# Seven-product MLP blocks: weight sums written later, products reordered, additions spread, transposes given a second PSUM pool

## The chip, the core and the metric

One core of a Trainium2 chip runs the whole program. The metric is device time in microseconds of one execution; the median of three runs is given, and beside it one further execution was profiled. Engines are named as in the profile: PE is the matrix engine (PEld its weight loads), DVE the vector engine, ACT the scalar engine, SP the engine whose queue issues the weight loads from HBM.

## The reference

A trunk of two layers on 256 tokens of width 2048. Each layer has a token mixer (differential attention in the first, a Mamba-2 mixer in the second) and then a squared-ReLU MLP with 8192 hidden units; both are pre-normed and added to the residual. The change touches the two MLPs only.

```python
def rms_norm(x, gain):
    y = xf * lax.rsqrt(jnp.mean(xf * xf, axis=-1, keepdims=True) + EPS)
    return y * gain
def sq_relu_mlp(h, w1, w2):
    return jnp.square(jax.nn.relu(h @ w1)) @ w2
...
for i in range(DEPTH):                      # DEPTH = 2
    hn = rms_norm(h, mixer_norm[i])
    h = h + (diff_attention(hn, ...) if i % 2 == 0 else mamba2_mixer(hn, ...))
    h = h + sq_relu_mlp(rms_norm(h, mlp_norm[i]), mlp_w1[i], mlp_w2[i])
```

All arrays are float32.

## The kernel before

**Precision.** Every operand of a matrix product is split in two: a rounded high part (a cast on ACT) and the rest (a subtraction on DVE). `split_weights` does it for a 128x1024 tile of weights (lines 158 and 159), `split_pair` for activations (lines 263 and 264). A product then takes high by high, high by low and low by high, three matmuls where one would do. So each 512 KB tile of weights costs one load (SP), one cast (ACT, L158), one subtraction (DVE, L159) and 12 or 6 wide matmuls.

**Stages.** Attention, first MLP (`mlp0`, about 405 to 1075 us in the profile), Mamba-2 mixer, second MLP (`mlp1`, about 1760 us to the end). The hidden layer of an MLP is made in eight chunks of 1024 columns. `MLP_KINDS` is "sSSSSSSS": chunk 0 is made by plain blocks (`blocks`, lines 169 and 173), the other seven by `seven`, a Strassen-Winograd product of 2x2 blocks with seven half-size products in place of eight. `seven` reads four quarters of a weight chunk, in four row parts i each: `src[0]` is B11, `src[1]` B12, `src[2]` B22, `src[3]` B21. It works in three loops over i:

- first loop: P1 = A11 B11 and P5 = S1 (B11 - B12), the sum kept in a tile `wsum` (L569);
- second loop: P7 = S3 (B22 - B12) (L579), P3 = S4 B22, P6 = S2 (B22 + wsum) (L584);
- third loop: P2 = A12 B21 and P4 = A22 (wsum - B21) (L600).

Each product of one i is six wide matmuls (L557 and L559) into one PSUM bank. The banks come from three pools: `aux` has three banks, `aux1` one, and `mm` (called by `bank()`) four, which the second matrix uses. After the second loop five additions (L587 to L591) form three of the four output quarters from P1, P3, P5, P6 and P7, and four ACT instructions (L593, L594) apply the squared ReLU to two of them; after the third loop L603 and L604 finish the other two, with L606 and L607.

**Second matrix.** `expand` turns a finished chunk `u` into transposed, split activations: for chunk 0 four splits only, for the others four groups of four PE transposes (L656), each group into an `aux` bank, and then a split out of that bank. `token_steps` multiplies them by tiles of w2 (L238, L240).

**Order.** The MLP goes in four quarters q. While quarter q is multiplied by w2, the two chunks of quarter q+1 are made: after each w2 step some `yield`s of the generator `seven` are taken (`work`, `rate`). The first two chunks are made together (`both(0, ...)`): four yields of `blocks`, then the two in turn. I call that stage the first pair. Small work hangs in a queue (`side`), of which `side.tick()` runs one step. Within an engine a scheduler of the framework settles the final order of instructions from this recording, so a line that is written later need not stand later. All waits between engines are by semaphores, and a tile's buffer (`raw` 5, `w` 4, `wsum` 4) is used again when its last reader is done.

## Time and profile before

| | |
|---|---|
| median of three runs | 2449.77 us (2448.08 to 2452.68) |
| the profiled execution | 2449.62 us, of which the span of the profile is 2447.9 us |
| granted PE clock | 1.0 throughout |
| PE busy | 2434.1 us, 99% of the span |
| DVE busy | 2098.2 us, 86% |
| ACT busy | 1535.6 us, 63% |
| DMA | 500.54 MB, mean 204 GB/s |

How to read it: a row of a group of instructions gives the engine, the operation, tiles written and read, the shape, the count, busy time in us and mean time of one in ns, and then the idle time of the engine just ahead of these instructions with what ended it. A row of the timeline gives start and duration in us, and in brackets idle time and its releaser. Matmuls overlap: a 512-column matmul is recorded with 0.39 us but the next can start 0.23 us after it. So I speak of PE by the distance of two starts, not by its busy time.

### The profile page before, as it was taken

What the parts mean: (1) busy time and instruction counts of PE and PEld (TensorE: products, weight loads), DVE (VectorE), ACT (ScalarE), POOL (GpSimd) and SP (SyncE); (2) the same over time, 40 slices, a digit from 0 to 9 for tenths busy, and PEclk for the clock granted to TensorE, in tenths of its full rate; (3) what the DMA queues carried; (4) which work ended last, traced back from release to release, by engine and by line L of the source; (5) the groups of instructions that cost most, each with busy time, mean ns of one, the idle gap of its engine ahead of it and who ended that gap; (6) DMA issues with size and microseconds to landing.
All of it is one profiled execution on the core that took longest, in us unless ns stands there. A gap on an engine that the chain in (4) does not pass through costs nothing.

```text
span 2447.9 us, 32626 instructions
## 1 busy us (share of the span) xinstructions
PE 2434.1 (99%) x12050; PEld 2038.8 (83%) x12050; DVE 2098.2 (86%) x2591; ACT 1535.6 (63%) x2154; POOL 1.2 (0%) x8
## 2 busy tenths in 40 slices
PE   9999999999999999999999999999999999999999
PEld 8888888878888788888888888888887888878887
DVE  6988879999998999568886887887899999899964
ACT  7666656666666666456776575775666666666653
POOL 0000000000000000000000000000000000000000
PEclk9999999999999999999999999999999999999999
DMA  8545555667667676556565556556566766776764
GB/s 287 164 157 175 167 175 194 208 232 243 230 208 230 221 231 218 191 177 211 190 198 196 174 198 199 166 189 191 190 218 220 239 229 203 238 232 206 233 205 147
DMA packets 140192, 500.54 MB, mean 204 GB/s; under 512 B 15648, under 2 KB 15840, under 8 KB 140032
## 3 DMA queue, kind: packets, MB, share of 16 engines
q1 hardware_dynamic: 137312, 489.75, 61.3%
q10 hardware_dynamic: 2720, 8.71, 1.0%
q8 instruction: 94, 1.54, 0.2%
q14 instruction: 66, 0.54, 0.1%
HBM read 496.24 MB, written 2.16 MB: 204 GB/s over the span
## 4 chain that ended last, share of the span: by engine, by line
PE 70%; DVE 18%; DMA 7%; issue 4%; ACT 1%; DVEq 0%; SPq 0%; ACTq 0%
PE pp L238 21%; PE pp L169 16%; DVE w L159 11%; PE pp L240 10%; PE pp L173 9%; PE aux L557 6%; DMA raw<-in_w11s 3%; DMA raw<-in_w10s 3%; PE aux L559 3%; DVE wsum L569 1%; DVE wsum L600 1%; DVE raw L579 1%; PE aux L878 1%; DVE h L716 1%; ACT w L158 1%
## 5 line engine op out<-in xcount | busy, mean ns | idle before, releaser
L159 DVE TENSOR_TENSOR w<-raw,w 128x1024 fp32r<-128x1024 f32 x858 | 1034.6, 1219 | 196.1 <-ACT w L158 193.5
L158 ACT CAST w<-raw 128x1024 fp32r<-128x1024 f32 x858 | 892.7, 1052 | 493.4 <-PE pp L238 316.3
L238 PE MATMUL pp<-w,act 128*128 128x512 f32 x3072 | 983.1, 391 | 0.7 <-ACT w L158 0.7
L238 PEld LDWEIGHTS pp<-w,act 128*128 128x128 f32 x3072 | 575.4, 188 | 121.7 <-ACT w L158 1.5
L240 PE MATMUL pp<-w,act 128*128 128x512 f32 x1536 | 598.5, 390 | 0.0
L169 PE MATMUL pp<-act,w 128*128 128x512 f32 x2000 | 489.0, 392 | 0.0
L169 PEld LDWEIGHTS pp<-act,w 128*128 128x128 f32 x2000 | 366.4, 188 | 72.6 <-issue 1.0
L240 PEld LDWEIGHTS pp<-w,act 128*128 128x128 f32 x1536 | 288.3, 188 | 58.0
L557 PE MATMUL aux<-w,sa 128*128 128x512 f32 x896 | 300.3, 392 | 5.2 <-DVE act L264 1.7
L173 PEld LDWEIGHTS pp<-act,w 128*128 128x128 f32 x2000 | 258.3, 191 | 11.0 <-issue 0.9
L173 PE MATMUL pp<-act,w 128*128 128x256 f32 x2000 | 266.8, 284 | 0.0
L158 ACT CAST w<-wsum 128x1024 fp32r<-128x1024 f32 x168 | 176.9, 1053 | 114.6 <-PE pp L238 43.8
L557 PE MATMUL aux<-w,act 128*128 128x512 f32 x672 | 228.8, 394 | 0.8 <-ACT w L158 0.3
L159 DVE TENSOR_TENSOR w<-wsum,w 128x1024 fp32r<-128x1024 f32 x168 | 204.8, 1219 | 1.9 <-ACT w L158 1.5
L557 PEld LDWEIGHTS aux<-w,sa 128*128 128x128 f32 x896 | 167.4, 188 | 44.3 <-DVE w L159 4.7
L559 PE MATMUL aux<-w,sa 128*128 128x512 f32 x448 | 175.2, 391 | 0.0
L557 PEld LDWEIGHTS aux<-w,act 128*128 128x128 f32 x672 | 124.8, 188 | 32.2 <-DVE w L159 6.2
L559 PE MATMUL aux<-w,act 128*128 128x512 f32 x336 | 131.4, 391 | 0.0
L559 PEld LDWEIGHTS aux<-w,sa 128*128 128x128 f32 x448 | 84.2, 188 | 16.7
L569 DVE TENSOR_TENSOR wsum<-raw 128x1024 f32<-128x1024 f32 x56 | 68.4, 1222 | 21.4 <-DMA raw<-in_w10s 11.5
L579 DVE TENSOR_TENSOR raw<-raw 128x1024 f32<-128x1024 f32 x56 | 68.5, 1222 | 20.4 <-DMA raw<-in_w11s 11.4
L600 DVE TENSOR_TENSOR wsum<-wsum,raw 128x1024 f32<-128x1024 f32 x56 | 68.0, 1220 | 7.4 <-DMA raw<-in_w11s 3.9
(218 smaller groups left out, 1736.0 us busy)
## 6 DMA issues: line engine op xcount, KB each, us to landing
raw<-in_w SPq DMA_DIRECT2D x288, 512.0 KB, 4.4
raw<-in_win SPq DMA_DIRECT2D x160, 512.0 KB, 4.1
raw<-in_w10s SPq DMA_DIRECT2D x140, 512.0 KB, 4.3
raw<-in_w11s SPq DMA_DIRECT2D x140, 512.0 KB, 4.3
raw<-in_wout SPq DMA_DIRECT2D x64, 512.0 KB, 4.1
raw<-in_qk SPq DMA_DIRECT2D x56, 512.0 KB, 4.3
raw<-in_wv SPq DMA_DIRECT2D x32, 512.0 KB, 4.2
raw<-in_wo SPq DMA_DIRECT2D x32, 512.0 KB, 4.2
```

The source lines that it names most:

```text
L158: S.copy(out=wh[:, s], in_=raw[:, s])
L159: V.tensor_tensor(out=wl[:, s], in0=raw[:, s], in1=wh[:, s].bitcast(F32), op=ALU.subtract)
L169: PE.matmul(acc, lhsT=wk, rhs=acts[k0 + k], start=(start and k == 0), stop=False)
L173: PE.matmul(acc[:, 0, :], lhsT=wk, rhs=acts[k0 + k][:, 0, :], start=False, stop=(stop and k == 7))
L238: PE.matmul(pp[t], lhsT=act[:, 0, tok], rhs=m, start=(s + i + k == 0), stop=(s == n - 1 and i + k == 2))
L240: PE.matmul(pp[t], lhsT=act[:, 1, tok], rhs=m, start=False, stop=False)
L557: PE.matmul(pp, lhsT=ah, rhs=m, start=(i + kp + j == 0), stop=(i == 3 and kp + j == 2))
L559: PE.matmul(pp, lhsT=al, rhs=m, start=False, stop=False)
L569: V.tensor_tensor(out=a[i], in0=b11, in1=b12, op=ALU.subtract)
L579: V.tensor_tensor(out=b12, in0=b22, in1=b12, op=ALU.subtract)
L600: V.tensor_tensor(out=a[i], in0=a[i], in1=b21, op=ALU.subtract)
L716: V.scalar_tensor_tensor(out=h[:, t, cols(j)], in0=pp[t], scalar=r2[:, t:t + 1], in1=h[:, t, cols(j)], op0=ALU.mult, op1=ALU.add)
```

## The change

It has five parts, all in `seven`, `expand`, `both` and the loop around them:

1. In the first loop the sum B11 - B12 is written after P1 and its yield, not ahead of them.
2. The second loop goes P3, P7, P6 instead of P7, P3, P6, and loads B22 ahead of B12. The tile that is first loaded is thus cast as it is; both sums are written after P3.
3. The third to fifth addition after the second loop, with their ACT instructions, move into the third loop (`late`), one part after each P4 of i = 0, 1, 2; the sum from P2 follows after i = 3, and only that from P4 stays behind the loop.
4. The splits of chunk 0 (`expand(0)`) are queued when `blocks` is finished, not at the start of the second matrix.
5. In `expand`, the second group of each two takes a bank of the pool `mm`. For the last quarter, whose splits go to another pool (`place`), all groups stay in `aux`.

No instruction is added or removed but for this order; the loads are the same, with B22 and B12 swapped.

```diff
@@ seven, first loop
             w = split_weights(b11)
+            product(p1, A11, w, i)
+            yield
             V.tensor_tensor(out=a[i], in0=b11, in1=b12, op=ALU.subtract)
-            product(p1, A11, w, i)
-            yield
             product(p5, S1, split_weights(a[i]), i)
@@ second loop
-            b12, b22 = load(src[1, i]), load(src[2, i])
+            b22, b12 = load(src[2, i]), load(src[1, i])
+            product(p3, S4, split_weights(b22), i)
+            yield
             V.tensor_tensor(out=b12, in0=b22, in1=b12, op=ALU.subtract)
+            V.tensor_tensor(out=a[i], in0=b22, in1=a[i], op=ALU.add)
             product(p7, S3, split_weights(b12), i)
             yield
-            product(p3, S4, split_weights(b22), i)
-            yield
-            V.tensor_tensor(out=a[i], in0=b22, in1=a[i], op=ALU.add)
             product(p6, S2, split_weights(a[i]), i)
             yield
         V.tensor_tensor(out=u[:, 0, 1], in0=p6, in1=u[:, 0, 0], op=ALU.add)
         V.tensor_tensor(out=u[:, 1, 0], in0=p7, in1=u[:, 0, 1], op=ALU.add)
-        V.tensor_tensor(out=u[:, 0, 1], in0=u[:, 0, 1], in1=u[:, 1, 1], op=ALU.subtract)
-        V.tensor_tensor(out=u[:, 0, 1], in0=p3, in1=u[:, 0, 1], op=ALU.add)
-        V.tensor_tensor(out=u[:, 1, 1], in0=u[:, 1, 0], in1=u[:, 1, 1], op=ALU.subtract)
-        for t in range(2):
-            S.activation(u[:, t, 1], u[:, t, 1], AF.Relu)
-            S.activation(u[:, t, 1], u[:, t, 1], AF.Square)
+        def relu2(t, n): ...      # Relu and Square of u[:, t, n]
+        def u4(): ...             # u01 = u01 - u11
+        def c12(): ...            # u01 = p3 + u01, relu2(0, 1)
+        def c22(): ...            # u11 = u10 - u11, relu2(1, 1)
+        late = [u4, c12, c22]
@@ third loop
             product(p4, A22, split_weights(a[i]), i)
-            yield
-        V.tensor_tensor(out=u[:, 0, 0], in0=p2, in1=u[:, 0, 0], op=ALU.add)
+            if i < 3:
+                late[i]()
+            else:
+                V.tensor_tensor(out=u[:, 0, 0], in0=p2, in1=u[:, 0, 0], op=ALU.add)
+                relu2(0, 0)
+            yield
         V.tensor_tensor(out=u[:, 1, 0], in0=u[:, 1, 0], in1=p4, op=ALU.subtract)
-        for t in range(2):
-            S.activation(u[:, t, 0], u[:, t, 0], AF.Relu)
-            S.activation(u[:, t, 0], u[:, t, 0], AF.Square)
+        relu2(1, 0)
@@ expand
-                    ax = aux().rearrange("p (a b) -> p a b", a=2)
+                    ax = aux().rearrange("p (a b) -> p a b", a=2) if i == 0 or place is not None else bank()
@@ both, and the loop over q
+            side.add(early)       # early = expand(0, hid), between chunk 0's last step and the rest of chunk 1
             yield from b
...
+            if q == 0:
+                side.add(expand(1, hid))
```

What the scheduler makes of it, at three places (line numbers behind the change are those of the changed kernel: 571, 581, 582 and 611 are the sums 569, 579, 584 and 600; 616 and 619 are 603 and 604; 669 is 656).

DVE in the second loop of the first pair of the second MLP, before; `raw_15829` and `raw_15909` are the second tile loaded of their i, `raw_15907` the first:

```order
L584 TENSOR_TENSOR wsum_15635<-raw_15829,wsum_15635 128x1024
L159 TENSOR_TENSOR w_15867<-raw_15829,w_15867 128x1024
L579 TENSOR_TENSOR raw_15907<-raw_15909,raw_15907 128x1024
L159 TENSOR_TENSOR w_15877<-wsum_15635,w_15877 128x1024
L159 TENSOR_TENSOR w_15888<-raw_15886,w_15888 128x1024
L159 TENSOR_TENSOR w_15912<-raw_15907,w_15912 128x1024
```

and behind the change, at the same place:

```order
L582 TENSOR_TENSOR wsum_15635<-raw_15827,wsum_15635 128x1024
L159 TENSOR_TENSOR w_15868<-raw_15829,w_15868 128x1024
L582 TENSOR_TENSOR wsum_15691<-raw_15907,wsum_15691 128x1024
L159 TENSOR_TENSOR w_15877<-wsum_15635,w_15877 128x1024
L159 TENSOR_TENSOR w_15888<-raw_15886,w_15888 128x1024
L159 TENSOR_TENSOR w_15911<-raw_15907,w_15911 128x1024
L581 TENSOR_TENSOR raw_15909<-raw_15907,raw_15909 128x1024
```

The sum that needs the second tile of the next i has gone from ahead of the split of `wsum_15635` to behind three further splits; in its place stands a sum that needs only the first tile.

DVE at the end of the first pair of the first MLP, before (`u_3753` is chunk 0, `u_3951` chunk 1, `wsum_4581` the first sum of chunk 2, which P5 waits for):

```order
L159 TENSOR_TENSOR w_4552<-wsum_4104,w_4552 128x1024
L222 TENSOR_TENSOR u_3753<-pp_4466,u_3753 128x256
L687 RECIPROCAL r2_3752<-ms_103 128x2
L159 TENSOR_TENSOR w_4582<-raw_4577,w_4582 128x1024
L569 TENSOR_TENSOR wsum_4581<-raw_4577,raw_4579 128x1024
L603 TENSOR_TENSOR u_3951<-aux_4409,u_3951 128x512
L604 TENSOR_TENSOR u_3951<-u_3951,aux_4410 128x512
L264 TENSOR_TENSOR act_4592<-u_3753,act_4592 128x2x256
L159 TENSOR_TENSOR w_4595<-wsum_4581,w_4595 128x1024
```

and behind it:

```order
L264 TENSOR_TENSOR act_4591<-u_3753,act_4591 128x2x256
L159 TENSOR_TENSOR w_4552<-wsum_4104,w_4552 128x1024
L222 TENSOR_TENSOR u_3753<-pp_4460,u_3753 128x256
L159 TENSOR_TENSOR w_4582<-raw_4577,w_4582 128x1024
L616 TENSOR_TENSOR u_3951<-aux_4402,u_3951 128x512
L571 TENSOR_TENSOR wsum_4581<-raw_4577,raw_4579 128x1024
L619 TENSOR_TENSOR u_3951<-u_3951,aux_4403 128x512
L264 TENSOR_TENSOR act_4604<-u_3753,act_4604 128x2x256
L159 TENSOR_TENSOR w_4595<-wsum_4581,w_4595 128x1024
```

One split of chunk 0 (L264) and one addition (L616) now stand ahead of the sum for P5 (L571).

PE at the start of quarter 1 of the first MLP, before (`u_4574` is a finished chunk, `w_5900` is for P1, `w_5883` for P5):

```order
L656 MATMUL aux_5875<-ident_71,u_4574 128x128 x4
L557 MATMUL aux_5853<-w_5900,act_3594 128x512
L559 MATMUL aux_5853<-w_5900,act_3594 128x512
L557 MATMUL aux_5853<-w_5900,act_3603 128x512
L559 MATMUL aux_5853<-w_5900,act_3603 128x512
L557 MATMUL aux_5853<-w_5900,act_3594 128x512
L557 MATMUL aux_5853<-w_5900,act_3603 128x512
L238 MATMUL pp_5923<-w_5927,act_5880 128x512
L238 MATMUL pp_5924<-w_5927,act_5880 128x512
L557 MATMUL aux_5854<-w_5883,sa_3784 128x512
```

and behind it:

```order
L669 MATMUL pp_5874<-ident_71,u_4574 128x128 x4
L557 MATMUL aux_5854<-w_5883,sa_3784 128x512
L559 MATMUL aux_5854<-w_5883,sa_3784 128x512
L557 MATMUL aux_5854<-w_5883,sa_3832 128x512
L559 MATMUL aux_5854<-w_5883,sa_3832 128x512
L557 MATMUL aux_5854<-w_5883,sa_3784 128x512
L557 MATMUL aux_5854<-w_5883,sa_3832 128x512
L557 MATMUL aux_5853<-w_5900,act_3594 128x512
L559 MATMUL aux_5853<-w_5900,act_3594 128x512
```

P5 with its bank follows the transposes at once, because the second group no longer holds the third bank of `aux`; two further groups of transposes (`aux_5909`, `pp_5914`) then stand together behind P1. Over a quarter the transposes of two chunks stand in four places on PE, where they stood in seven.

Elsewhere: in the third loop the additions stand one by one between splits; but at the end of quarter 0, ahead of the second split of a `wsum`, stand three sums L611 where two L600 stood.

More of the change, by code (lines that the diff above doesn't have):

```diff
@@ L568, in seven @@
             w = split_weights(b11)
-            V.tensor_tensor(out=a[i], in0=b11, in1=b12, op=ALU.subtract)
             product(p1, A11, w, i)
             yield
+            V.tensor_tensor(out=a[i], in0=b11, in1=b12, op=ALU.subtract)
             product(p5, S1, split_weights(a[i]), i)
@@ L588, in seven, with relu2, u4, c12 @@
         V.tensor_tensor(out=u[:, 1, 0], in0=p7, in1=u[:, 0, 1], op=ALU.add)
-        V.tensor_tensor(out=u[:, 0, 1], in0=u[:, 0, 1], in1=u[:, 1, 1], op=ALU.subtract)
-        V.tensor_tensor(out=u[:, 0, 1], in0=p3, in1=u[:, 0, 1], op=ALU.add)
-        V.tensor_tensor(out=u[:, 1, 1], in0=u[:, 1, 0], in1=u[:, 1, 1], op=ALU.subtract)
-        for t in range(2):
-            S.activation(u[:, t, 1], u[:, t, 1], AF.Relu)
-            S.activation(u[:, t, 1], u[:, t, 1], AF.Square)
+        def relu2(t, n):
+            S.activation(u[:, t, n], u[:, t, n], AF.Relu)
+            S.activation(u[:, t, n], u[:, t, n], AF.Square)
+        def u4():
+            V.tensor_tensor(out=u[:, 0, 1], in0=u[:, 0, 1], in1=u[:, 1, 1], op=ALU.subtract)
+        def c12():
+            V.tensor_tensor(out=u[:, 0, 1], in0=p3, in1=u[:, 0, 1], op=ALU.add)
+            relu2(0, 1)
+        def c22():
+            V.tensor_tensor(out=u[:, 1, 1], in0=u[:, 1, 0], in1=u[:, 1, 1], op=ALU.subtract)
+            relu2(1, 1)
+        late = [u4, c12, c22]
         p2, p4 = aux(), aux()
@@ L660, in expand, with both @@
                     yield
-        def both(q, share):
+        def both(q, share, early=None):
             if not share:
@@ L683, in mlp @@
         side.add(sums_of(), slow=True)
-        for _ in both(0, 28 / 12 if kinds[:2] == "sS" else 1.0):
+        hid = []
+        for _ in both(0, 28 / 12 if kinds[:2] == "sS" else 1.0, expand(0, hid)):
             pass
@@ L688, in mlp @@
         for q in range(4):
-            if q < 3:
+            if q == 0:
+                side.add(expand(1, hid))
+            elif q < 3:
                 hid = []
```

## Prediction

> **What bounds the kernel now.** I read the page first, then the groups of PE by form, the busy time by stretches of the MLPs, and last the timeline around each place where two PE starts lie too far apart.
>
> ```profile
> PE 2434.1 (99%) x12050; PEld 2038.8 (83%) x12050; DVE 2098.2 (86%) x2591; ACT 1535.6 (63%) x2154; POOL 1.2 (0%) x8
> PE 70%; DVE 18%; DMA 7%; issue 4%; ACT 1%; DVEq 0%; SPq 0%; ACTq 0%
> L238 PEld LDWEIGHTS pp<-w,act 128*128 128x128 f32 x3072 | 575.4, 188 | 121.7 <-ACT w L158 1.5
> L557 PE MATMUL aux<-w,sa 128*128 128x512 f32 x896 | 300.3, 392 | 5.2 <-DVE act L264 1.7
> ```
>
> PE is busy almost without a break, and the chain that ended last runs 70% on it. Only what stops PE can be won. A matmul is recorded with 392 ns, but in the fence on the additions below the starts 802.09, 802.32 and 802.55 lie 0.23 us apart, so I measure stops as start to start less 0.227. The Trainium skill ("Perfetto Trace Analysis", section Identifying the Most-Contended Engine) says to judge PE by the busy share of its weight loads, not of its matmuls. By that, 17% of the span (some 410 us) would be open. The trace does not bear that out: a weight load takes 188 ns of a step of 227, which is 83%, so 83% is a full stream, and I give that reading no chance.
>
> ```profile
> 427.00:490.00 63.00, 62.36 (x310) 52.15 (x309) 62.99 (x72) 44.39 (x56) 0.00 (x0) 1.00 0.64 207
> 655.00:826.00 171.00, 170.31 (x761) 139.11 (x760) 157.73 (x151) 106.56 (x117) 0.00 (x0) 1.00 0.69 225
> 1785.00:1848.00 63.00, 61.28 (x306) 51.25 (x304) 61.59 (x70) 42.85 (x54) 0.00 (x0) 1.00 0.64 202
> ```
>
> The columns are the length, then busy time of PE, PEld, DVE, ACT and POOL, the clock, the DMA share and GB/s. In the first pair of the first MLP (first row) DVE works 62.99 of 63 us: there DVE is the bound, and PE only lives on its lead. In the second MLP's first pair it lacks 1.41 us. In the quarters it has some 13 us of 171 to spare, and PE is the bound.
>
> **The change part by part.** The sum is against the profiled execution, 2449.62 us; the median of the runs, 2449.77, is 0.15 above it.
>
> *Second loop (part 2).* B22 is split as it lands, so the sum of two loaded tiles no longer has to wait for the second.
>
> ```profile
> L579 DVE TENSOR_TENSOR raw<-raw 128x1024 f32<-128x1024 f32 x56 | 68.5, 1222 | 20.4 <-DMA raw<-in_w11s 11.4 <-DMA raw<-in_w10s 8.7
> 1800.53 1.23 DVE L579 TENSOR_TENSOR raw<-raw 128x1024 f32<-128x1024 f32 x1 [1.41 <-DMA raw<-in_w11s]
> 1801.11 0.39 PE L559 MATMUL aux<-w,sa 128*128 128x512 f32 x1
> 1801.67 1.22 DVE L159 TENSOR_TENSOR w<-wsum,w 128x1024 fp32r<-128x1024 f32 x1
> 1802.94 0.73 PE L557 MATMUL aux<-w,sa 128*128 128x512 f32 x2 [1.45 <-DVE w L159]
> ```
>
> DVE idles 20.4 us in all at this sum. Once, in the second MLP's first pair, it decides: DVE waits 1.41 us for a load, the split of `wsum` queues behind, and PE stops 1802.94 - 1801.11 - 0.23 = 1.60 us. In the new order a sum of the tile that landed earlier stands there, and the late one comes three splits (3.4 us by starts 1.13 apart) later. DVE bounds this stage, so the stage gains what DVE does: **-1.4**. In the first MLP's pair DVE has no idle time that could go: 0. In the quarters the rest of the 20.4 is DVE's spare time: 0 on PE, but DVE gets about 1.4 us per `seven` (20.4/14) ahead. The queue of loads keeps its length and its releases but for two or three; its range is nothing to +1 each way.
>
> *First sums (part 1) and early splits (part 4), end of the first pair.* The late line changes little in the order of the first loop. At the chunk's end it does.
>
> ```profile
> 487.78 1.22 DVE L569 TENSOR_TENSOR wsum<-raw 128x1024 f32<-128x1024 f32 x1
> 488.92 0.68 DVE L603 TENSOR_TENSOR u<-aux,u 128x512 f32<-128x512 f32 x1
> 489.09 1.05 ACT L158 CAST w<-wsum 128x1024 fp32r<-128x1024 f32 x1 [0.43 <-DVE wsum L569]
> 489.52 0.68 DVE L604 TENSOR_TENSOR u<-u,aux 128x512 f32<-128x512 f32 x1
> 490.19 0.51 PE L557 MATMUL aux<-w,sa 128*128 128x512 f32 x1 [0.76 <-DVE u L604]
> 491.10 1.14 ACT L607 ACTIVATE u<-u 128x512 f32<-128x512 f32 x2
> 491.77 0.33 PE L656 MATMUL aux<-ident,u 128*128 128x128 f32 x1 [0.36 <-ACT u L607]
> 492.14 1.98 ACT L158 CAST w<-raw 128x1024 fp32r<-128x1024 f32 x2
> 493.23 0.50 PE L557 MATMUL aux<-w,act 128*128 128x512 f32 x1 [0.17 <-ACT w L158]
> ```
>
> The row at 490.19 names L604, but the cast at 489.09 ends at 490.14: P5 waits for the cast of its sum. Behind the change two instructions of 0.60 us each (488.92 to 489.52) stand ahead of that sum on a full DVE, so P5 starts at about 491.4, 1.2 later. In return one squared ReLU runs before, and the stops at 491.77 and 493.23 go: four matmuls and a transpose to 492.5, two matmuls to 493.0, the next cast done at about 492.9, its four matmuls and three transposes to 494.3. Before, the same work ends at 493.23 + 0.11 + 4 x 0.227 = 494.3. So **0** for both MLPs; ends +1.2 each (nothing behind gets shorter) and -0.9 each (P5 not later). Should the cover fail, P5 is what is late next.
>
> *Banks (part 5).*
>
> ```profile
> 659.86 0.62 PE L238 MATMUL pp<-w,act 128*128 128x512 f32 x2
> 660.54 0.50 PE L557 MATMUL aux<-w,sa 128*128 128x512 f32 x1
> 660.88 0.39 PE L559 MATMUL aux<-w,sa 128*128 128x512 f32 x1
> 673.24 0.39 PE L240 MATMUL pp<-w,act 128*128 128x512 f32 x1
> 674.07 0.66 PE L656 MATMUL aux<-ident,u 128*128 128x128 f32 x4 [0.44 <-DVE act L264]
> 825.61 0.39 PE L557 MATMUL aux<-w,act 128*128 128x512 f32 x1
> 830.32 1.28 DVE L264 TENSOR_TENSOR act<-aux,act 128x512 fp32r<-128x512 f32 x2
> 831.05 0.50 PE L557 MATMUL aux<-w,sa 128*128 128x512 f32 x1 [1.19 <-DVE act L264]
> 2189.15 0.51 PE L557 MATMUL aux<-w,sa 128*128 128x512 f32 x1 [0.54 <-DVE act L264]
> ```
>
> Into quarter 1, P5 waits for a bank that the splits L264 free: 660.54 - 659.86 - 2 x 0.227 = 0.23, then 0.11 for the restart (660.88 - 660.54 = 0.34 in place of 0.23). At 674.07 a group of transposes waits 0.60, and 0.08. With the fourth bank P5 follows at once; the next groups need the first L264, which ends at about 660.5 while PE gets there at about 661.2. So -1.0 in this MLP, and the same in the other: **-2.1**. Into quarter 2 DVE is later: L264 runs at 830.32. P5 no longer waits (1.36 and 0.71: the idle time and 0.17 of overlap). The work behind 825.61 in the new order is P1's last matmuls (1.4), eight transposes (0.8), P5 (1.4), P1 (1.4), so at 830.5 the third group asks for the `aux` bank that L264 frees at about 831.0; two groups (0.9) and eight matmuls (1.85) later, at 833.7, the fifth asks for one that is freed only after further splits, by my estimate at about 834.5. Counted to the end of the same work that leaves 0.4 in the first MLP and 0.3 in the second: **-0.7**, with ends -2.3 (no new wait) and +1. A bank of `mm` is lent for the time of one split. None of the first matmuls of a column block waits for the residual additions L716 in the new order, so the lending costs nothing unless the splits are over 3 us late. The Trainium skill ("Perfetto Trace Analysis", section Optimizing Tensor Performance) says that independent groups should rotate through different banks, so that the evacuation of one lies beside the next group's matmuls. By that rule alone all of these waits would go, -4.4 in place of -2.8, and the sum below would be 1.6 lower; the row at 830.32 speaks against it, since the splits themselves are queued on DVE.
>
> *Transposes in fewer places.*
>
> ```profile
> 665.47 0.60 PE L656 MATMUL aux<-ident,u 128*128 128x128 f32 x4
> 665.83 0.47 PE L559 MATMUL aux<-w,sa 128*128 128x512 f32 x1
> 666.14 0.39 PE L557 MATMUL aux<-w,sa 128*128 128x512 f32 x1
> ```
>
> The first matmul behind a group takes 0.31 from start to start, 0.08 more than the others. Four such places fewer in quarters 0 and 1 of each MLP (quarter 2 is in the sum above): 8 x 0.08 = **-0.6**.
>
> *Additions (part 3).*
>
> ```profile
> 800.54 0.69 DVE L590 TENSOR_TENSOR u<-aux,u 128x512 f32<-128x512 f32 x1
> 801.14 0.69 DVE L591 TENSOR_TENSOR u<-u 128x512 f32<-128x512 f32 x1
> 801.74 1.22 DVE L159 TENSOR_TENSOR w<-wsum,w 128x1024 fp32r<-128x1024 f32 x1
> 802.09 0.39 PE L559 MATMUL aux<-w,act 128*128 128x512 f32 x1
> 802.32 0.39 PE L557 MATMUL aux<-w,act 128*128 128x512 f32 x1
> 802.55 0.39 PE L559 MATMUL aux<-w,act 128*128 128x512 f32 x1
> 803.02 0.50 PE L557 MATMUL aux<-w,act 128*128 128x512 f32 x1
> ```
>
> Two additions ahead of the split of a `wsum` make P4 stop 0.47 - 0.23 = 0.24 us, and 0.11 for the restart: 0.35. I found six such stops of 0.16 to 0.34 before a split L159 in the quarters, together 2.1 with their restarts. Spread out, the additions cover them, if the sums L611 that now stand ahead of splits don't take their place. I count four of six: **-1.5**, with ends -2.1 and 0.
>
> Sum: -1.4 + 0 - 2.1 - 0.7 - 0.6 - 1.5 = -6.3. That is 2443.3 for the profiled execution and **2443.5** for the median, 0.26% faster. About 0.2% (4.9 us) is what a measurement can tell from no change.
>
> **Rivals.**
>
> *The waits move along DVE.* DVE works 158 of 171 us in a quarter, and what it gives PE at one place it is late with at the next. Then only the lost idle time of the first pair and the rarer restarts remain (-1.4 - 0.6), and perhaps a third of the other 4.3: 2449.8 - 3.4 = 2446.4, no change that can be told. For it: at the first pair's end just this happens. Against it: in the quarters PE, not DVE, is the bound, and DVE gains 1.4 us per `seven`.
>
> *The sums of the third loop get ahead of the splits.* At the end of quarter 0 three sums L611 stand ahead of a split where two L600 stood; the sum takes 1.14 us by its starts. If every one of the 12 `seven` in quarters were late by that on PE, it would cost 13.7, less 6.3: 2457. It is slower by over 0.2% only when ten of the twelve pass the full delay on; with one addition (0.6) gone from the same place the net delay is 0.5, and the 1.4 that DVE gains at L579 covers it. That speaks against.
>
> *More goes.* All stops in the two MLPs that L557 and L656 show, with their restarts, add up to some 11 us; with the rarer restarts 2438 would be the best. That would need the first pair to be free of DVE, which its row of 62.99 denies.
>
> *The early split does not do what it says.* No step of the side queue is taken between its old and new place; only one L264 moves. This changes nothing in the sum.
>
> **How the numbers follow.** The forecast, 2440 to 2446: 0.6, nearly all of it faster, a little just within 0.2% (beyond 2444.9). Waits that move along DVE, 2446 to 2450: 0.27. The sums ahead of the splits, or another mishap of that size: 0.08. More than forecast, below 2440: 0.05. Range 2438.5 to 2450.0, the second case whole: above it I leave the slower case (0.08), below it most of the last (0.05). Faster 0.60, same 0.33, slower 0.07.
>
> **What the profile would show.** Right: in the second MLP's first pair no stop of PE of over 1 us and no idle time of DVE at L581; the group L581 with far less idle time than 20.4; P5 into quarters 1 and 2 starts behind the transposes without a wait; the rows of L557 lose most of their 5.2 us. Still there: a stop at each end of the first pair, P5 now about 1.2 later against DVE, and waits of L669 for L264 into quarter 2. Wrong: if P5 into quarter 1 waits for its cast, if L611 has a large idle time ahead of it for its load, or if matmuls of L238 wait for L733.

## The result and the profile after

The changed kernel takes 2458.42 us (median of 8 executions, 2455.03 to 2465.66), the kernel before 2450.49 (8, 2448.08 to 2453.54): ratio 1.0035, 95% interval 1.0026 to 1.0044. It is 7.9 us slower, where 6.3 us faster was forecast. Measured once more (h1 below) the ratio was 1.0027 (1.0017 to 1.0037). The profiled execution, 2455.03 us with a span of 2453.0, was the fastest of its eight, so its trace shows 5.1 of the 7.9 us.

From the page of the changed kernel, the busy times and the chain that ended last:

```profile
PE 2434.8 (99%) x12050; PEld 2038.0 (83%) x12050; DVE 2099.0 (86%) x2591; ACT 1536.4 (63%) x2154; POOL 1.2 (0%) x8
PE 74%; DVE 15%; DMA 6%; issue 3%; ACT 2%; DVEq 0%; ACTq 0%; SPq 0%
```

The busy times are those of the kernel before to within 0.8 us, so nothing is done more slowly; work only waits longer. The groups of DVE's sums, first the three of the kernel before that the prediction did not quote (its L579 idled 20.4 us), then the four of the changed kernel. The last numbers are the idle time of DVE just ahead of them, and on whom:

```profile
L569 DVE TENSOR_TENSOR wsum<-raw 128x1024 f32<-128x1024 f32 x56 | 68.4, 1222 | 21.4 <-DMA raw<-in_w10s 11.5 <-DMA raw<-in_w11s 9.9
L584 DVE TENSOR_TENSOR wsum<-raw,wsum 128x1024 f32<-128x1024 f32 x56 | 68.2, 1218 | 0.0
L600 DVE TENSOR_TENSOR wsum<-wsum,raw 128x1024 f32<-128x1024 f32 x56 | 68.0, 1220 | 7.4 <-DMA raw<-in_w11s 3.9 <-DMA raw<-in_w10s 3.5
```

```profile
L571 DVE TENSOR_TENSOR wsum<-raw 128x1024 f32<-128x1024 f32 x56 | 68.5, 1223 | 23.0 <-DMA raw<-in_w10s 12.0 <-DMA raw<-in_w11s 11.0
L582 DVE TENSOR_TENSOR wsum<-raw,wsum 128x1024 f32<-128x1024 f32 x56 | 68.5, 1223 | 14.7 <-DMA raw<-in_w10s 8.5 <-DMA raw<-in_w11s 5.7
L611 DVE TENSOR_TENSOR wsum<-wsum,raw 128x1024 f32<-128x1024 f32 x56 | 68.4, 1222 | 14.3 <-DMA raw<-in_w11s 7.9 <-DMA raw<-in_w10s 6.1
L581 DVE TENSOR_TENSOR raw<-raw 128x1024 f32<-128x1024 f32 x56 | 68.4, 1221 | 7.0 <-DMA raw<-in_w11s 3.6 <-DMA raw<-in_w10s 3.4
```

The sum for P7 does wait less, 7.0 for 20.4. But the sum for P6 (L582, before it was L584), which had waited for nothing, now waits 14.7, and that of the third loop 14.3 for 7.4. The four together wait 59.0 us (56.4 in the second profile), where they waited 49.2.

What one such wait does, from the timelines while chunk 7 is made. First DVE in the kernel before, where these sums and splits follow each other without a pause:

```profile
939.26 1.22 DVE L584 TENSOR_TENSOR wsum<-raw,wsum 128x1024 f32<-128x1024 f32 x1
940.40 3.49 DVE L159 TENSOR_TENSOR w<-raw,w 128x1024 fp32r<-128x1024 f32 x3
943.81 1.22 DVE L579 TENSOR_TENSOR raw<-raw 128x1024 f32<-128x1024 f32 x1
944.95 1.22 DVE L584 TENSOR_TENSOR wsum<-raw,wsum 128x1024 f32<-128x1024 f32 x1
```

Then the changed kernel, DVE and PE:

```profile
942.62 1.23 DVE L582 TENSOR_TENSOR wsum<-raw,wsum 128x1024 f32<-128x1024 f32 x1 [1.24 <-DMA raw<-in_w10s]
943.77 3.49 DVE L159 TENSOR_TENSOR w<-raw,w 128x1024 fp32r<-128x1024 f32 x3
...
950.39 1.23 DVE L611 TENSOR_TENSOR wsum<-wsum,raw 128x1024 f32<-128x1024 f32 x1 [0.86 <-DMA raw<-in_w10s]
951.53 3.49 DVE L159 TENSOR_TENSOR w<-raw,w 128x1024 fp32r<-128x1024 f32 x3
```

```profile
945.04 0.96 PE L557 MATMUL aux<-w,sa 128*128 128x512 f32 x3 [0.52 <-DVE w L159]
952.81 0.96 PE L557 MATMUL aux<-w,sa 128*128 128x512 f32 x3 [0.67 <-DVE w L159]
```

L582 of the next step needs only B22, so in the new order it stands ahead of two splits of this step. B22 of the next step has not landed; DVE stands still for 1.24 us with the splits behind it, and PE stops at the low part of the split (0.68 us by starts). At 952 the same happens with L611 (0.83).

Where the 5.1 us lie, by the times at which the same (n-th) matmul of L169 or L238 starts in both traces; both MLPs added, in us against the kernel before. A is from the start of an MLP to 65 us into quarter 0 (409 to 555 us, and 1767 to 1913), B the rest of quarter 0, the passages, quarter 1 and chunk 6 (to 907, and 2265), C chunk 7 and the rest (to 1037, and the end):

```
                                     A       B       C    before the MLPs   whole span
changed                            +2.9    -2.6    +5.6        -0.8            +5.1
changed, second profile (h1)       +4.0    -5.6    +5.6        -0.7            +3.3
```

### The profile page after: what moved, and what is told of

It reads as the page before. It is cut to its first block, busy times and chain, and to the rows that moved or that the text cites. A ratio compares the mean times of both kernels' runs of the same rounds, so it can differ in the third digit from the quotient of the medians.

```text
span 2453.0 us, 32588 instructions
## 1 busy us (share of the span) xinstructions
PE 2434.8 (99%) x12050; PEld 2038.0 (83%) x12050; DVE 2099.0 (86%) x2591; ACT 1536.4 (63%) x2154; POOL 1.2 (0%) x8
## 4 chain that ended last, share of the span: by engine, by line
PE 74%; DVE 15%; DMA 6%; issue 3%; ACT 2%; DVEq 0%; ACTq 0%; SPq 0%
PE pp L238 22%; PE pp L169 16%; PE pp L240 11%; DVE w L159 9%; PE pp L173 9%; PE aux L557 7%; PE aux L559 4%; DMA raw<-in_w11s 3%; DMA raw<-in_w10s 3%; ACT w L158 1%; DVE wsum L582 1%; DVE raw L581 1%; PE aux L895 1%; DVE wsum L611 1%; PE pp L354 1%
## 5 line engine op out<-in xcount | busy, mean ns | idle before, releaser
L238 PE MATMUL pp<-w,act 128*128 128x512 f32 x3072 | 984.1, 391 | 1.2 <-ACT w L158 0.7
L238 PEld LDWEIGHTS pp<-w,act 128*128 128x128 f32 x3072 | 574.8, 188 | 123.1 <-ACT w L158 1.9
L169 PE MATMUL pp<-act,w 128*128 128x512 f32 x2000 | 488.8, 392 | 0.0
L169 PEld LDWEIGHTS pp<-act,w 128*128 128x128 f32 x2000 | 366.3, 188 | 72.6 <-issue 1.0
L557 PE MATMUL aux<-w,sa 128*128 128x512 f32 x896 | 302.2, 394 | 8.4 <-DVE w L159 4.5
L557 PE MATMUL aux<-w,act 128*128 128x512 f32 x672 | 226.4, 391 | 0.6 <-DVE u L587 0.6
L557 PEld LDWEIGHTS aux<-w,sa 128*128 128x128 f32 x896 | 166.2, 188 | 52.7 <-DVE w L159 14.5
L557 PEld LDWEIGHTS aux<-w,act 128*128 128x128 f32 x672 | 125.8, 188 | 29.0 <-issue 1.6
L571 DVE TENSOR_TENSOR wsum<-raw 128x1024 f32<-128x1024 f32 x56 | 68.5, 1223 | 23.0 <-DMA raw<-in_w10s 12.0
L582 DVE TENSOR_TENSOR wsum<-raw,wsum 128x1024 f32<-128x1024 f32 x56 | 68.5, 1223 | 14.7 <-DMA raw<-in_w10s 8.5
L611 DVE TENSOR_TENSOR wsum<-wsum,raw 128x1024 f32<-128x1024 f32 x56 | 68.4, 1222 | 14.3 <-DMA raw<-in_w11s 7.9
```

Of the source, the lines that this page charges most:

```text
L169: PE.matmul(acc, lhsT=wk, rhs=acts[k0 + k], start=(start and k == 0), stop=False)
L238: PE.matmul(pp[t], lhsT=act[:, 0, tok], rhs=m, start=(s + i + k == 0), stop=(s == n - 1 and i + k == 2))
L557: PE.matmul(pp, lhsT=ah, rhs=m, start=(i + kp + j == 0), stop=(i == 3 and kp + j == 2))
L571: V.tensor_tensor(out=a[i], in0=b11, in1=b12, op=ALU.subtract)
L582: V.tensor_tensor(out=a[i], in0=b22, in1=a[i], op=ALU.add)
L611: V.tensor_tensor(out=a[i], in0=a[i], in1=b21, op=ALU.subtract)
```

## Experiments

All are against the kernel before on the same chip; "ratio" is the time over that of the kernel before with its 95% interval.

### The parts alone

**e1**, the changed kernel with the second loop as before; **e2**, the kernel before with the new second loop; **e4**, the kernel before with only the banks.

```diff
e1 = changed, second loop: load b12, b22; sum, P7; P3; sum, P6      (as before)
e2 = before,  second loop: load b22, b12; P3; both sums, P7; P6     (as changed)
e4 = before,  expand: ax = aux() if i == 0 or place is not None else bank()
```

> All of the change but the second loop, which goes P7, P3, P6 as before. Theory (the new order lets sums that wait for a load stand on DVE ahead of splits that PE needs; that costs about 10 us, and the banks give back about 3.4): about 2446.5 us, 2444 to 2449, and the DVE sums wait for loads some 49 us in all, as before, instead of 59. Rival A (the spread additions push the sums of the third loop ahead of splits): 2456 or more. Rival B (the lent bank holds up the second matrix): 2455 or more.

> The kernel before with only the second loop in the new order and B22 loaded first. Theory: slower than before by 8 to 11 us, about 2460, with the stops of PE in the quarters behind splits of loaded tiles, and about 59 us of DVE waits for loads. Rivals A and B: 2448 to 2451, since neither additions nor banks are touched.

> The kernel before with only the second bank pool for every second group of transposes. From the two traces the passages between quarters are 1.8 and 1.6 us shorter in the changed kernel. Theory: 2447, 2445.5 to 2448.5, faster by 3.4. Rival B: slower than before.

e1: 2449.3 beside 2448.74, ratio 1.0002 (0.9993 to 1.0011), waits of the sums 45.0 us. e2: 2454.61, 1.0024 (1.0015 to 1.0033), waits 60.0. e4: 2450.61, 1.0006 (0.9997 to 1.0015). So the new second loop costs (5.9 us of median): the loss is there with it alone, and gone without it.

The rest of the change brings nothing instead of the 3.4 us I expected of the banks. Part of that may be another effect, told in the last section: in e1's trace the PE clock halves twice for 3.4 us, and the mean clock of all its 11 executions is 0.999, while the changed kernel has 1.0 in 17 of 18.

In e2 the stops stand where the changed kernel has them, in both MLPs (2304 and 2312 in the second):

```profile
L582 DVE TENSOR_TENSOR wsum<-raw,wsum 128x1024 f32<-128x1024 f32 x56 | 68.3, 1222 | 18.8 <-DMA raw<-in_w10s 10.2 <-DMA raw<-in_w11s 8.3
L600 DVE TENSOR_TENSOR wsum<-wsum,raw 128x1024 f32<-128x1024 f32 x56 | 68.0, 1221 | 14.8 <-DMA raw<-in_w11s 8.1 <-DMA raw<-in_w10s 6.7
```

```profile
944.45 0.96 PE L557 MATMUL aux<-w,sa 128*128 128x512 f32 x3 [1.04 <-DVE w L159]
952.37 0.96 PE L557 MATMUL aux<-w,sa 128*128 128x512 f32 x3 [0.83 <-DVE w L159]
```

By stretches e2 has A +1.1, B -1.7, C +6.2, and e4 A +1.5, B -2.0, C +1.0. In e4 the passages gain (B), but a new stop of 0.96 stands 12 us behind the first pair, at 505.25 and again at 1862.18. Its timeline, DVE and PE:

```profile
501.65 0.68 DVE L264 TENSOR_TENSOR act<-aux,act 128x512 fp32r<-128x512 f32 x1
502.25 0.68 DVE L264 TENSOR_TENSOR act<-pp,act 128x512 fp32r<-128x512 f32 x1
502.85 1.21 DVE L569 TENSOR_TENSOR wsum<-raw 128x1024 f32<-128x1024 f32 x1
```

```profile
505.25 0.50 PE L557 MATMUL aux<-w,sa 128*128 128x512 f32 x1 [0.80 <-ACT w L158]
```

The lent bank (`pp`) lets the transposes of chunk 1 run earlier, so two of their splits now stand ahead of the sum that P5 waits for, 1.2 us of a DVE that is still full. **e5** lends only from chunk 2 on:

```diff
+            lend = c > 1 and place is None
-                    ax = aux()...
+                    ax = bank() if i and lend else aux()...
```

> The kernel before, with the second bank pool lent for the transposes of chunks 2 to 5 only, not for chunk 1, whose splits fall where DVE is still full behind the first pair. Theory (the gain of the banks at the passages between quarters is real, but for chunk 1 the earlier splits stand ahead of the sum that P5 waits for and cost 0.96 us in each MLP): 2.5 to 4 us faster than before, no stop of P5 12 us behind the first pair. Rival (what the banks give is taken back anywhere on a full DVE): no change, as when all chunks borrow.

2446.73 beside 2448.86, ratio 0.9993 (0.9984 to 1.0001); the stop at 505 is gone, A is -0.2. The median gained 2.1 us, less than expected, and the interval just holds 1: likely, not shown. Nor does the trace show it. Its execution took 2450.0, nearly the longest of its eleven: the passages into quarters 1 and 2 are 3.6 us shorter together, and as much is lost again in the rest of B, at small stops of PE that wait for splits. So the rival of this run, that DVE hands the gains on, is not excluded. **e6**, the additions alone, and **e8**, both:

> The kernel before with only the additions spread over the third loop. The term of the prediction: 1.5 us faster. From the run without the new second loop I now expect about 1 us, nearly all of it in the last quarters made (0.3 and 0.5 there). Rival A (the sums of the third loop get ahead of splits by it): 3 us or more slower.

> The kernel before with the second bank pool for chunks 2 to 5 and the additions spread. Theory: the sum of both alone, 3.5 to 5 us faster than before, 0.15 to 0.2%. Rival: DVE hands the two gains on and less than 2 us are left.

e6: 2449.3, 0.9995 (0.9986 to 1.0005); e8: 2446.88, 0.999 (0.9981 to 0.9999). The additions don't harm, against rival A, and with the banks the two are just faster.

**e7**, the kernel before with only the sum of the first loop written after P1:

> The kernel before with only the sum of the first loop written after P1. The term of the prediction: 0, since at the end of the first pair one stop grows by what two others lose. From the run without the new second loop less the run with the banks alone I now expect 1.5 us in the first MLP and 0.9 in the second, some 2.4 us slower, all between the end of the first pair and 65 us behind it.

2455.49, ratio 1.0026 (1.0017 to 1.0036): 6.6 us slower for a part that I had set at 0, and nearly three times what I then expected. The parts don't add up: e1 contains this part and is only 0.6 us slower, so 6.6 is not its price inside the changed kernel. Its timeline, PE, at the end of the first pair:

```profile
491.16 0.50 PE L557 MATMUL aux<-w,sa 128*128 128x512 f32 x1 [1.96 <-ACT w L158]
...
493.06 0.63 PE L557 MATMUL aux<-w,act 128*128 128x512 f32 x1
493.49 0.63 PE L559 MATMUL aux<-w,act 128*128 128x512 f32 x1
493.92 0.63 PE L557 MATMUL aux<-w,act 128*128 128x512 f32 x1
```

P5 starts at 491.16, close to the 491.4 of the prediction. But then the matmuls are 0.43 us apart instead of 0.23 (the last section says why). And the lateness doesn't end at 494.3, where my count ended: a split L264 now stands ahead of a sum and waits itself, and PE's transposes behind it.

```profile
499.61 0.69 DVE L264 TENSOR_TENSOR act<-aux,act 128x512 fp32r<-128x512 f32 x1 [1.51 <-ACT act L263]
500.22 1.22 DVE L571 TENSOR_TENSOR wsum<-raw 128x1024 f32<-128x1024 f32 x1
```

```profile
500.35 0.44 PE L656 MATMUL aux<-ident,u 128*128 128x128 f32 x2 [0.70 <-DVE act L264]
```

### Mending by place

I then thought that three places made the loss: L582, the first late sum, and the bank for chunk 1. **e3** is the changed kernel with L582 held behind L581 by an edge of order in DVE's queue, **e9** the same on e2. **e10** is e7 with the first step as before, **e11** the changed kernel with that step as before, **e12** all three mended.

```diff
e3, e9:    tc.keep_in_program_order(V.tensor_tensor(out=a[i], in0=b22, in1=a[i], op=ALU.add))
e10, e11:  if i == 0: the sum ahead of P1; else behind P1 and its yield
```

> The changed kernel, with the sum for P6 held behind the sum for P7 of the same step in the queue of DVE (an edge of order alone, no wait is added), so that it no longer stands ahead of the splits of the step before. Theory: most of the loss goes, about 2450, 2446 to 2454, and the idle time of DVE at this sum (14.7 us) becomes small. Rivals A and B: 2457 to 2460, as the changed kernel. If what counts is that loads land late and not who waits for them, the idle time moves to the sum for P7 and the time stays at 2458.

> The kernel before with only the new second loop, and the sum for P6 held behind the sum for P7 of its step in the queue of DVE. Theory (the whole loss of the new loop comes from that sum, which waits for the first tile of the next step ahead of splits of this step): nearly all of the 5.9 us goes, 2447 to 2451 beside 2449 of before, and no stops of about 1 us at some 945, 952, 2304 and 2312 us. Rival (the loads as such land later in the new order, whoever waits for them): 2453 or more, with the idle time of DVE now at the sum for P7.

> The kernel before with the sum of the first loop written late in steps 1 to 3 only. Theory (the 6.6 us of the late sum come from its first step alone: at the end of the first pair P5 waits over 2 us, which in one MLP or both also halves the granted clock of PE for some 4 us, and DVE hands the lateness on through the next 25 us): no change, 2448 to 2450.5, granted clock 1.0 there. Rival (late sums cost in every chunk): 2453 or more.

> The changed kernel with only the first sum of each first loop written ahead of P1 again. Theory: its losses are two and separate, so what is left is that of the second loop: 3 to 6 us less than the changed kernel, a ratio of 1.001 to 1.0025 to before. Rival (one loss only, that of the second loop): as the changed kernel, 1.0035.

> The changed kernel mended at all three places: first sum of each first loop ahead of P1, the sum for P6 held behind that for P7, the second bank pool for chunks 2 to 5 only. Theory: faster than before, 2443 to 2447 beside 2449, since the gains of the banks and of the additions stay (together 2 to 2.5 us as measured alone) and the second MLP's first pair loses its stop of 1.6 us. Rival: DVE hands the gains on, 2448 or more.

e3: 2452.59 beside 2448.74, ratio 1.0013 (1.0004 to 1.0022). e9: 2453.14 beside 2449.47, 1.0018 (1.0009 to 1.0026). e10: 2455.63, 1.0026 (1.0015 to 1.0037). e11: 2458.4, 1.0038 (1.0023 to 1.0053). e12: 2453.61, 1.0015 (1.0006 to 1.0024).

Most of it missed: only e3 came out inside its range, and in e9, e10, e11 and e12 the rival came true. In e3 and e9 L582 waits 0.0, but L581 then waits 21.4 and 22.8: the stops at 945 and 952 are gone, while half of the loss or more stays. Where it lies is open. In e9 C is still +3.4, with stops at other places; e3's profiled execution took 2446.53, 6 us less than its median, so its trace (C +0.7, 3.1 us shorter than the kernel before in all) doesn't contain the loss. In e10 P5 is on time and the loss is no smaller. Of 6.2 us in its trace 4.1 lie in A, the first of them 8 us on, and 2.3 in B:

```profile
499.05 0.44 PE L659 MATMUL aux<-ident,u 128*128 128x128 f32 x2 [1.17 <-DVE act L264]
```

So no single place carries the loss. What the runs that lose in stretch A have in common is DVE's idle time there. In the first MLP (409 to 555 us) DVE idles 2.9 us before; with 4.2 the changed kernel is 2.1 us later there, with 5.5 e10 2.9, with 6.0 e7 3.4, with 6.7 e12 3.9, while e8 with 2.8 is 0.3 earlier. That is roughly one microsecond for each one more of idle time (farthest off is e11: 6.1, and 4.5 later; in e7, e11 and e12 the PE clock also halves there). In the second MLP the relation is looser: the changed kernel is 0.8 later with 4.4 us of idle time, where the kernel before has 4.5.

### Doses: where DVE is the bound

**g1, g2, g3**: the kernel before with the same four DVE instructions more in the first loop of one chunk of each MLP.

```diff
             product(p5, S1, split_weights(a[i]), i)
+            if more:                                  # chunk 2, 4 or 7
+                V.tensor_tensor(out=a[i], in0=a[i], in1=a[i], op=ALU.max)
```

> The kernel before with one more DVE instruction per step in the first loop of chunk 2 (the maximum of the sum tile with itself, which changes nothing; 4 x 1.14 = 4.6 us of DVE in each MLP, 9.1 in all). Chunk 2 is the first made in quarter 0, 490 to 575 us, where DVE of the kernel before has no idle time until 565. Theory (there DVE is still the bound): 7 to 9 us slower, one to one. Rival (the prediction's premise, in the quarters PE is the bound): 0 to 2 us.

> The same four instructions in chunk 4, the first made in quarter 1, 655 to 740 us, where DVE of the kernel before idles some 7 us. Theory: 0 to 3 us slower, since idle time takes up most of it. Rival (any DVE time anywhere in the MLPs costs one to one): 9 us.

> The same four instructions in chunk 7, the last made, 905 to 985 us, where DVE idles 3.2 us up to the end of the chunk and the changed kernel lost 2.7 us with 1.5 us more of idle time. Theory (a tight stretch too): 3 to 7 us slower. Rival (PE is the bound there): 0 to 2.

9.1 us of DVE in chunk 2 cost 9.5 us (2457.95 beside 2448.46, ratio 1.0041, 1.0027 to 1.0055), and the trace has it in stretch A (+9.6). In chunk 4 they cost nothing (2445.82, 0.9994, 0.9985 to 1.0003), in chunk 7 3.2 us (2451.7, 1.0011, 1.0002 to 1.0021). The kernel before shows why, by stretches of the first MLP (chunks 2, 4, and 7 are made in these):

```profile
490.00:565.00 75.00, 74.27 (x331) 60.47 (x332) 74.43 (x73) 48.56 (x57) 0.00 (x0) 1.00 0.68 230
655.00:740.00 85.00, 84.50 (x388) 69.39 (x387) 80.64 (x80) 55.49 (x62) 0.00 (x0) 1.00 0.68 219
905.00:985.00 80.00, 80.00 (x360) 66.04 (x359) 74.45 (x72) 50.99 (x56) 0.00 (x0) 1.00 0.72 235
```

and the changed kernel, the first and the last of these:

```profile
490.00:565.00 75.00, 73.42 (x325) 59.07 (x326) 72.68 (x71) 46.94 (x54) 0.00 (x0) 1.00 0.70 229
905.00:985.00 80.00, 78.76 (x347) 63.86 (x346) 74.02 (x70) 50.29 (x55) 0.00 (x0) 1.00 0.69 222
```

DVE (third busy time) is full not only in the first pair but for 75 us behind it: 74.43 of 75. There, by dose g1, a microsecond of DVE is a microsecond of PE, and the changed kernel lets DVE stand still 2.3 of the 75 (before: 0.6). In quarter 1 there is room. While chunk 7 is made DVE is busy 74.45 of 80, and about a third of the dose comes through.

### Holding the sums where there is room

If sums that wait for loads stand too early, they should be held back, as in **g4**: e8 with the first loop's sum held directly behind the split of its own tile. **h2** holds it from chunk 3 on only, since the sum for P5 of chunk 2 lies in the full stretch.

```diff
+            d = V.tensor_tensor(out=a[i], in0=b11, in1=b12, op=ALU.subtract)
+            if hold:                                  # g4: always; h2: c > 2
+                tc.keep_in_program_order(d)
```

> The kernel before with the second bank pool for chunks 2 to 5, the additions spread, and the sum of the first loop held directly behind the split of its own tile in the queue of DVE. Theory: no sum waits for a load ahead of other splits any more in the first loop, so its 21.4 us of idle time shrink; 2443 to 2447, at least as good as without the hold. Rival (held back, the sum is followed at once by its own split, which then waits for the cast): slower than without the hold, 2449 or more.

> As the run with the sum of the first loop held, but held in chunks 3 to 7 only; second bank pool for chunks 2 to 5 and additions spread as there. Theory (in the DVE-full stretch behind the first pair a held sum makes P5 wait over 2 us; elsewhere DVE has the time): 2 to 3 us less than with the hold in all chunks, a ratio of 0.9975 to 0.9985 to before, no stop of P5 over 1 us at some 494 us. Rival (the gain in quarter 1 came with the loss ahead of it): as before the edit, 0.9988 to 0.999.

g4: 2445.28 beside 2448.46, ratio 0.9988 (0.998 to 0.9997), A +3.2, B -8.4, C +1.7. h2: **2441.93 beside 2449.04, ratio 0.9975 (0.9965 to 0.9985)**, A -0.7, B -8.8, C +1.5: faster than both kernels. Its sums (L613 is that of the third loop):

```profile
L581 DVE TENSOR_TENSOR raw<-raw 128x1024 f32<-128x1024 f32 x56 | 68.3, 1219 | 9.0 <-DMA raw<-in_w11s 4.6 <-DMA raw<-in_w10s 4.4
L569 DVE TENSOR_TENSOR wsum<-raw 128x1024 f32<-128x1024 f32 x56 | 68.2, 1218 | 6.5 <-DMA raw<-in_w11s 3.6 <-DMA raw<-in_w10s 2.9
L613 DVE TENSOR_TENSOR wsum<-wsum,raw 128x1024 f32<-128x1024 f32 x56 | 68.1, 1217 | 6.7 <-DMA raw<-in_w11s 3.5 <-DMA raw<-in_w10s 3.1
```

L569 waits 6.5 us where it waited 21.4, and the sums 22.2 together (L586, the sum for P6, 0.0):

```
                    first loop    P7     P6   third loop   together   ratio
before                    21.4  20.4    0.0          7.4       49.2
changed                   23.0   7.0   14.7         14.3       59.0   1.0035
e1 old second loop        20.2  18.4    0.0          6.4       45.0   1.0002
e2 new second loop        21.6   4.8   18.8         14.8       60.0   1.0024
e3 L582 held              24.1  21.4    0.0          6.7       52.2   1.0013
e7 late first sum         23.3  22.1    0.0          9.0       54.4   1.0026
e9 e2, L582 held          26.8  22.8    0.0          8.7       58.3   1.0018
g4 first sum held          0.0  12.6    0.0          5.6       18.2   0.9988
h2 held from chunk 3       6.5   9.0    0.0          6.7       22.2   0.9975
```

The other runs, without the doses, have together: e8 49.2, e6 50.8, e5 51.5, e4 51.9, e10 54.4, h1 56.4, e12 59.9 and e11 69.5. The order of the sums of waits is roughly that of the times, each sum being from one execution only. Out of place are e7 and e10, slower than their waits say (they lose in the full stretch), e9 and e12, faster, and g4, which waits less than h2 but takes longer. In g4 P5 stops 2.3 us at the end of the first pair, in the full stretch, and six of its 11 executions have a mean clock of 0.999; these have a median of 2446.3, the others of 2443.8.

**h1**, the changed kernel again:

> The changed kernel once more, for a second profile. Theory: ratio of about 1.0035 again; whatever this profile has beyond the first lies in the stretches where DVE is full (behind the first pair up to 565 us and its like in the second MLP, and the quarter made last), where DVE idles more than in the first profile. Rival: the additional time is outside the two MLPs, or at PE's own steps.

2455.9 beside 2449.44, 1.0027 (1.0017 to 1.0037). A and C lose 4.0 and 5.6, so the two stretches are confirmed. This profiled execution (2453.21) is again the fastest of its kernel; what the slower ones have beyond it is in no trace and stays open.

## Why the prediction was wrong, step by step

**Second loop (-1.4, and "0 on PE, but DVE gets about 1.4 us per `seven`").** The named stop went: behind the change no stop in the first pair of the second MLP is over 0.24 us. What PE gained there was lost again further on: stretch A of the second MLP is 0.8 us longer. The term is wrong in sign, and its range of "nothing to +1 each way" too narrow. The step that failed is that DVE "gets about 1.4 us per `seven`" ahead: I freed DVE of L579's wait and didn't ask what the sum moved up, L582, waits for itself. I quoted its new place ("a sum that needs only the first tile") and took the tile as landed. It waits 14.7 us, the four sums together wait 9.8 us more than before, e2 costs 5.9 us, and 5.6 us of the changed kernel's trace lie in stretch C, where I had counted nothing.

**End of the first pair (0, ends -0.9 and +1.2 each).** P5 was foreseen at 491.4; in the changed kernel it starts at 490.46, and that with a program that is 0.8 us ahead at the start of this MLP:

```profile
490.46 0.50 PE L557 MATMUL aux<-w,sa 128*128 128x512 f32 x1 [1.48 <-ACT w L158]
509.91 0.50 PE L557 MATMUL aux<-w,sa 128*128 128x512 f32 x1 [0.25 <-ACT w L158]
534.15 0.73 PE L557 MATMUL aux<-w,sa 128*128 128x512 f32 x2 [0.82 <-DVE w L159]
```

The two other stops went, as foreseen. What failed is the end of the count: that the same work ends at 494.3 in both leaves out that DVE behind it is as full as before it. Under it lies the premise that in the quarters PE is the bound, read from 157.73 of 171 us of quarter 1. Quarter 0 begins with 75 us without room (74.43 of 75), where new stops stand at 509.91 and 534.15; e7, this part alone, costs 6.6 us, of which the halved clock, in eight of its nine executions, may have some 2. What it costs inside the changed kernel no run shows by itself. Dose g1 shows the rate, one to one.

**Banks (-2.1, -0.7, -0.6: -3.4).** Right into quarter 1, in part into quarter 2. P5 into quarter 1 follows the transposes without a wait (changed kernel, first two rows), and the wait into quarter 2 moved to L669, as foreseen (third row). But in the second MLP two such waits (last rows) stand where one of 0.54 stood:

```profile
658.77 0.60 PE L669 MATMUL pp<-ident,u 128*128 128x128 f32 x4
659.12 0.48 PE L557 MATMUL aux<-w,sa 128*128 128x512 f32 x1
...
834.11 0.66 PE L669 MATMUL aux<-ident,u 128*128 128x128 f32 x4 [0.53 <-DVE act L264]
...
2191.80 0.66 PE L669 MATMUL aux<-ident,u 128*128 128x128 f32 x4 [0.50 <-DVE act L264]
...
2195.26 0.66 PE L669 MATMUL aux<-ident,u 128*128 128x128 f32 x4 [0.53 <-DVE act L264]
```

Between the same matmuls the passages are 1.2 us shorter into quarter 1 in each MLP, and into quarter 2 0.6 shorter in the first MLP and 0.5 longer in the second: 2.5 in all, where 3.4 were forecast (3.2 in h1; 4.2 in e4, the banks alone). Missed was chunk 1, whose earlier splits cost 0.96 us in each MLP (e4). No matmul of L238 waits for the lent bank. The rule weighed in the prediction (the Trainium skill, "Perfetto Trace Analysis", section Optimizing Tensor Performance: rotate independent groups through different banks) is borne out where DVE has room; the third row and chunk 1 show that the splits themselves, queued on DVE, are the limit behind it.

**Additions (-1.5).** e6 is 0.9995 (0.9986 to 1.0005): compatible, not shown.

**The rivals.** *The sums of the third loop get ahead of the splits*, at 0.08, comes nearest: sums do stand ahead of splits that PE needs. But its cause was the three sums L611 that the spread additions leave in one place, and no run shows a cost of these: with the additions spread and the old second loop L611 waits only 6.4 (e1) and 7.6 us (e6), while e2, without the spread, has 14.8 at L600. What decided was the wait of L582, and that 2457 lies near 2458.42 is luck: it was made of twelve times the 1.14 us that a sum takes, less the gains, and not of waits for loads. I dismissed this rival with the 1.4 us that DVE was to gain, the very number that was wrong.

*The waits move along DVE*, at 0.27, has its mechanism in e4 and e5, where the passages get 4.2 and 3.6 us shorter and the traces as a whole don't, but it left no room for a loss. *The early split does nothing* holds as far as the program goes: part 4 alone leaves the order of the instructions of every engine as it was. No run has it alone.

**The signs.** No stop over 1 us in the first pair of the second MLP, L581 at 7.0 us for 20.4, and P5 into quarters 1 and 2 without a wait are all there, though the kernel is slower. The row of L557 on `sa` should have lost most of its 5.2 us and has more instead:

```profile
L557 PE MATMUL aux<-w,sa 128*128 128x512 f32 x896 | 302.2, 394 | 8.4 <-DVE w L159 4.5 <-ACT w L158 3.5
```

The sign that I named for "wrong", a large idle time ahead of L611, is there too (14.3 us).

## What to carry to other kernels

On an engine that works its queue in order, ask of every instruction that moves up what it waits for itself, since all that stands behind it waits too; freeing one wait is a gain only if the next instruction is ready. Look for a bound in short stretches and in every stage, not in the mean of one: the 92% of quarter 1 said nothing of quarter 0, which has 157.53 of 165 us as a whole (95%) and begins with 75 us at 99%. There each microsecond of DVE cost one of PE, as four harmless instructions showed when put there, and put elsewhere. Parts of a change that are each measured alone need not add up. What waits for loads is better held back where there is room: that gave some 5 us (e8 to h2), where moving it up cost 6 (e2). That h2 gains through these waits is argued from the table, not shown apart from all else that its new order moves.

## What the hardware showed that I had not expected

After P5's wait in e7 the granted clock of PE fell to half. Its stretches, with the clock as the third number from the end:

```profile
491.00:492.00 1.00, 0.84 (x4) 0.71 (x5) 1.00 (x2) 1.00 (x3) 0.00 (x0) 1.00 0.88 221
492.00:493.00 1.00, 1.00 (x5) 0.61 (x4) 1.00 (x3) 1.00 (x2) 0.00 (x0) 0.94 0.98 389
493.00:494.00 1.00, 1.00 (x4) 0.74 (x3) 1.00 (x1) 1.00 (x2) 0.00 (x0) 0.50 1.00 410
497.00:498.00 1.00, 1.00 (x6) 0.84 (x5) 1.00 (x1) 0.00 (x0) 0.00 (x0) 1.00 0.83 336
```

The clock stands at 0.50 from 492.9 to 496.3 us, 3.4 us, and the step of a matmul there is 0.43 us, so by estimate PE lost 1.7 us more behind this pause of 1.96 us. It isn't certain to happen: in the second MLP of the same execution a pause as long left the clock at 1.00, and in e1 both MLPs had it.

Over all kept traces, from 20 to 2430 us, nine pauses of PE of 1.87 to 2.13 us stand; at six of them the clock halved, each time for 3.4 us, and at none of the shorter ones (1.62 us and less) alone. A price shows within one kernel too: in e3, e12 and g4 the executions with a mean clock of 0.999 take 2.0 to 2.5 us more of median than those with 1.0 (in e11, three against three, 6.5), though what else differs in them is in no trace.

The Trainium skill ("TensorE: Matmul & The Clock Gate", section Part 1: The HAM clock gate) says that the clock halves after at least one idle window of about 3.4 us, windows that run freely. The half clock and the part of chance agree; the length doesn't, a pause of 2 us was enough here, and in e7 PE was busy 1.72 of the 3.4 us ahead of the half clock.

It isn't what made the change slower: 17 of the 18 executions of the changed kernel have a mean clock of 1.0, and e10 loses 6 us at a clock of 1.0 in every one.
